# Gated linear attention: decay sums held in both signs, one VectorE operation per level for differences and one for factors, none on GpSimd

## The chip, the core and the metric

The kernel runs on one core of a Trainium2 chip. The metric is the device time of one execution in microseconds (us). TensorE (PE) multiplies matrices, VectorE (DVE), ScalarE (ACT) and GpSimd (POOL) work element by element on 128 partitions, and SyncE (SP) issues most of the DMAs. The engines run side by side, each through its own queue in order, and wait for each other by semaphores.

## The reference, cut to what matters

The network has several layers of 256 tokens by 1024 columns: gated linear attention, a convolutional FFN, sparse attention, a second FFN, a mixer and an expert layer. Only the first is touched. It computes, in float32:

```python
def gla_mixer(h, w_in, w_alpha_up, b_alpha, g_out, w_o):      # H=4 heads, DK=128, DV=256, chunks of C=64
    q, k, v, r, a_low = jnp.split(h @ w_in, splits, axis=-1)
    log_a = log_sigmoid(a_low @ w_alpha_up + b_alpha) / 16.0
    ...
    def step(state, inp):
        q_, k_, v_, g_ = inp                                   # q_ already times DK ** -0.5
        b = jnp.cumsum(g_, axis=2)
        o_inter = einsum('bhtk,bhkv->bhtv', q_ * exp(b), state)
        diff = b[:, :, :, None, :] - b[:, :, None, :, :]
        decay = where(causal, exp(minimum(diff, 0.0)), 0.0)
        att = einsum('bhtk,bhsk,bhtsk->bhts', q_, k_, decay)
        o_intra = einsum('bhts,bhsv->bhtv', att, v_)
        b_last = b[:, :, -1:, :]
        new_state = state * exp(b_last) + einsum('bhsk,bhsv->bhkv', k_ * exp(b_last - b), v_)
        return new_state, o_inter + o_intra
    ...
    o = o * rsqrt(mean(o * o) + EPS) * g_out
    return (o * silu(r)) @ w_o
```

So the attention weight of token t on an earlier token s is the sum over the 128 key channels of q[t] k[s] exp(b[t] - b[s]), where b is the running sum of the log decays.

## The kernel before, in words

All weights are streamed from memory in units of 128x1024 floats. Each unit is brought by one DMA into one of 4 buffers `raw`. ScalarE rounds it into `whi` (line 273), VectorE takes the rest `wlo = raw - whi` (line 274), and TensorE multiplies with three matmuls for each piece (lines 284 to 286). There are 5 buffers `whi` and 5 `wlo`. Whatever VectorE does besides stands in the same queue as these subtractions.

`gla` first multiplies the 8 units of `gla_a`, which give k and q, kept transposed in the tile `qk` (line 731, one head at a time: channels on the partitions, tokens along the row, first the four heads of k, then those of q). Then come the 12 units of `gla_b`, in groups of 4 with a PSUM bank for each half of the tokens: units 4 to 7 give the second half of v, 8 to 15 give r.

Between these units stands the attention, as steps of a background generator. The decay sums `b` come from `decays` (scans at line 714). The pairs of tokens are then split into levels, with blocks of m = 128, 64, 32, 16, 8, 4, 2 and 1 tokens: at level m a token s in the first block of a pair of blocks meets a token t in the second one, and the decay between them is the product of two factors taken against the last token r of the first block. For each level,

- `decay(m)` takes two VectorE differences of 128x512 elements: `r - b` on first blocks (line 725), `b - r` on second blocks (line 726); ScalarE then takes the exponential of the whole 128x1024 tile (line 727);
- two GpSimd multiplications of 128x512 put k on first blocks (line 791) and q on second blocks (line 792);
- `products(m)` multiplies first by second blocks on TensorE (line 767 for m = 128, 774 for m = 64, 782 below), and copies the result into the matrix `att`, by ScalarE for the first two levels and by VectorE's copy with a mask (line 783) for the others and for the diagonal (m = 0, which needs no decay).

The differences run 2 levels ahead of the factors, and the products follow 3 levels behind them. When all levels are in `att`, it is multiplied with v (lines 807 and 808). Line 741 multiplies silu(r) with a gain, on GpSimd too.

The code names engines and buffers. The order within an engine's queue, and the waits, come from a scheduler that goes by its own costs, so a change of an operation's shape or engine can move its neighbours. The places touched are line 681 (the tile `b`), lines 692 to 697 (views), 714, 719 to 727, 741, and 790 to 792.

Of the kernel before, what the change touches and what calls it, by code (L numbers as in the profile page):

```python
# [13 lines left out]
AF = mybir.ActivationFunctionType  # L14
ALU = mybir.AluOpType
# [5 lines left out]
T = 256  # L21
# [166 lines left out]
class Net:  # L188
# [479 lines left out]
    def gla(self):  # L668
        nc = self.nc
        with ExitStack() as es:  # L670
            sp = self.pool("gla", es)
# [4 lines left out]
            gg = self.t(sp, [128, D])  # L676
# [1 line left out]
            self.strict = False  # L678
            xh, xl = self.xh, self.xl
            qk = self.t(sp, [128, 2, 4, T])  # L680
            b = self.t(sp, [128, 4, T])
            aT = self.t(sp, [16, T])
            att = self.t(sp, [128, 8, 128])
            attx = self.t(sp, [128, 4, 128])
            ones = self.t(sp, [128, T])
# [3 lines left out]
            levels = (128, 64) + MASKED  # L689
            AHEAD, LAG = 2, 3  # L690
            E = {}
            bf = b.rearrange("p h t -> p (h t)")
            kf = qk[:, 0].rearrange("p h t -> p (h t)")
            qf = qk[:, 1].rearrange("p h t -> p (h t)")

            def view(a, m):
                return a.rearrange("p (n u m) -> p n u m", u=2, m=m)

            def decays():
                z = self.t(sp, [128, 4, T])  # L700
                mn = self.t(sp, [128, 4, T])
                for h2 in range(2):
                    pz = self.ps()
                    for j in range(2):
                        h = 2 * h2 + j
                        zs = pz[:, j * T:(j + 1) * T]
                        nc.tensor.matmul(zs, up[:, h * 128:(h + 1) * 128], aT, start=True, stop=True)
                        nc.scalar.activation(z[:, h], zs, AF.Abs, bias=ba[:, h:h + 1])
                        nc.vector.tensor_scalar(mn[:, h], zs, ba[:, h:h + 1], 0.0, op0=ALU.add, op1=ALU.min)
                nc.scalar.activation(z, z, AF.Exp, scale=-1.0)  # L710
                nc.scalar.activation(z, z, AF.Ln, bias=1.0)
                nc.vector.tensor_sub(z, mn, z)
                for h in range(4):
                    nc.vector.tensor_tensor_scan(b[:, h], ones, z[:, h], 0.0, op0=ALU.mult, op1=ALU.add)
                yield
                for m in levels[:AHEAD]:
                    decay(m)
                    yield

            def decay(m):  # L720
                n = 512 // m
                e = E[m] = self.t(sp, [128, 1024])
                ev, bv = view(e, m), view(bf, m)
                r = bv[:, :, 0, m - 1:m].to_broadcast([128, n, m])
                nc.vector.tensor_sub(ev[:, :, 0], r, bv[:, :, 0])  # L725
                nc.vector.tensor_sub(ev[:, :, 1], bv[:, :, 1], r)
                nc.scalar.activation(e, e, AF.Exp, scale=1.0 / 16.0)

            def evac_a(i, p):
# [2 lines left out]
            v = self.t(sp, [128, 2, D])  # L732
            rg = self.t(sp, [128, 2, D])

            def evac_b(g, ps):
                for t in range(2):
                    s = slice((g % 2) * 512, (g % 2) * 512 + 512)
                    to, fn = (v, AF.Copy) if g < 2 else (rg, AF.Silu)
                    nc.scalar.activation(to[:, t, s], ps[t], fn, scale=self.rs[:, t:t + 1])
                    if g == 2:  # L740
                        nc.gpsimd.tensor_mul(rg[:, t, s], rg[:, t, s], gg[:, s])
            evac_b(0, self.rest())
            p = self.ps()
            self.unit_n(self.A["gla_n"], 32, xh, xl, p[:, :T])
            self.tick()
            nc.vector.tensor_copy(aT, p[32:48, :T])
            nc.vector.tensor_add(aT, p[:16, :T], aT)
            nc.vector.tensor_mul(aT, aT, self.rw[:16])
            self.bg.append(decays())
            self.run(self.gemm_w(self.A["gla_a"], xh, xl, T, evac_a))  # L750
            self.close_right()
# [6 lines left out]
            def products(m):  # L758

                if m == 0:  # L760
                    kk, qq = qk[:, 0], qk[:, 1]
                else:
                    kk = qq = E[m].rearrange("p (h t) -> p h t", h=4)
                if m == 128:
                    p = self.ps()
                    for h in range(4):
                        nc.tensor.matmul(p[:, h * 128:(h + 1) * 128], kk[:, h, :128], kk[:, h, 128:], start=True, stop=True)
                    nc.scalar.activation(attx.rearrange("p h t -> p (h t)"), p, AF.Copy)
                elif m == 64:
                    p = self.ps()  # L770
                    for t in range(2):
                        for h in range(4):
                            i, s = t * 4 + h, t * 128
                            nc.tensor.matmul(p[:64, i * 64:(i + 1) * 64], kk[:, h, s:s + 64], kk[:, h, s + 64:s + 128], start=True, stop=True)
                    nc.scalar.activation(att[:64, :, 64:], p[:64].rearrange("p (i t) -> p i t", i=8), AF.Copy)
                else:
                    mask = self.cc(f"m{m}", "cg") if m else self.ident
                    for t in range(2):
                        p = self.ps()
                        for h in range(4):  # L780
                            s = slice(t * 128, t * 128 + 128)
                            nc.tensor.matmul(p[:, h * 128:(h + 1) * 128], kk[:, h, s], qq[:, h, s], start=True, stop=True)  # L782
                        nc.vector.copy_predicated(att[:, t * 4:t * 4 + 4], mask[:, None, :].bitcast(U32).to_broadcast([128, 4, 128]),  # L783
                                                  p.rearrange("p (h t) -> p h t", h=4))

            def attention():
                for i, m in enumerate(levels):
                    if i + AHEAD < len(levels):
                        decay(levels[i + AHEAD])
                    ev = view(E[m], m)  # L790
                    nc.gpsimd.tensor_mul(ev[:, :, 0], ev[:, :, 0], view(kf, m)[:, :, 0])
                    nc.gpsimd.tensor_mul(ev[:, :, 1], ev[:, :, 1], view(qf, m)[:, :, 1])
                    if i >= LAG:
                        products(levels[i - LAG])
                    yield
                for m in levels[len(levels) - LAG:] + (0,):
                    products(m)
                    yield
                po, r = {}, {}
                for t in range(2):  # L800
                    for h2 in range(2):
                        p = po[t, h2] = self.ps()
                        for j in range(2):
                            h = 2 * h2 + j
                            o = p[:, j * 256:(j + 1) * 256]
                            if t:
                                nc.tensor.matmul(o, attx[:, h], v[:, 0, h * 256:(h + 1) * 256], start=True, stop=False)
                            nc.tensor.matmul(o, att[:, t * 4 + h], v[:, t, h * 256:(h + 1) * 256], start=not t, stop=True)
                            sq = self.t(sp, [128, 256], tag="sq", bufs=2)
                            nc.scalar.activation(sq, o, AF.Square, accum_out=ss[:, t * 4 + h:t * 4 + h + 1])  # L810
                    r[t] = self.root(sp, ss[:, 4 * t:4 * t + 4], 4, 1.0 / 256)
                    yield

                def heads(t, hs, by):
                    for h in hs:
                        s = slice(h * 256, (h + 1) * 256)
                        nc.vector.scalar_tensor_tensor(on[:, t, s], po[t, h // 2][:, (h % 2) * 256:(h % 2 + 1) * 256], r[t][:, h:h + 1],
                                                       by[:, s], op0=ALU.mult, op1=ALU.mult)
                for t in range(2):
                    heads(t, (0, 1), rg[:, t])  # L820
                    self.turn_half(on[:, t, :512], oh, ol, 0, t * 128)
                    yield
                for t in range(2):
                    heads(t, (2, 3), gg)
                yield

            self.bg.append(attention())
            self.run(self.gemm_t(self.A["gla_b"][4:8], xh, xl, self.TT, lambda g, ps: evac_b(1, ps)), lambda: self.tick(2))
            self.run(self.gemm_t(self.A["gla_b"][8:], xh, xl, self.TT, lambda g, ps: evac_b(g + 2, ps)))
            self.drain()  # L830
            for t in range(2):
# [1058 lines left out]
```

## Time and profile before

| | |
|---|---|
| median of 3 runs | 1677.5 us (1676.87 to 1677.64) |
| the profiled execution, its own time | 1678.32 us |
| its span, first to last instruction | 1676.5 us |
| granted TensorE clock, mean of the span | 0.995 |
| TensorE busy | 1645.5 us (98%) |
| VectorE busy | 1271.6 us (76%) |
| ScalarE busy | 870.0 us (52%) |
| GpSimd busy | 99.3 us (6%) |

Start times in the views are counted from the start of the span. The busy time of one instruction includes some overlap with the next one on its engine: where several follow each other without a gap, the distance between their starts is what one of them costs the queue. In the views, unnamed tiles are all called `v`. "Releaser" is what ended an idle time.

### The profile page before, as it was taken

The page shows a single profiled execution, that of the slowest core. Times are in us where ns is not written, and L with a number is a line of the kernel's source. Part 1 is how long each engine was busy: PE and PEld are TensorE (multiplying, and loading weights), DVE is VectorE, ACT ScalarE, POOL GpSimd, SP SyncE. Part 2 cuts the span into 40 slices and gives each one's busy share as a digit, 9 for nine tenths or more (in the row PEclk, how much of TensorE's full clock was granted, in tenths as well). Part 3 has the DMA queues.
Part 4 walks back from the last instruction along what each step waited for, and adds up shares of the span by engine and source line. Part 5 has one row for each costly group of instructions (what it writes and reads, how often), then busy time and mean ns, then how long its engine had stood idle before and what let it go on. Part 6 is the DMA issues. An engine that isn't in the chain of part 4 may idle for free.

```text
span 1676.5 us, 28909 instructions
## 1 busy us (share of the span) xinstructions
PE 1645.5 (98%) x11363; PEld 1467.6 (88%) x11363; DVE 1271.6 (76%) x2168; ACT 870.0 (52%) x1379; POOL 99.3 (6%) x106
## 2 busy tenths in 40 slices
PE   9899999999999999999999999999999999999999
PEld 7688998898788998789779999999988998778887
DVE  6956987598857986599668889999955449985554
ACT  7445665456646665467455445433444444344443
POOL 0710000011101000210010000000000000000000
PEclk9899999999999999999999999999999999999999
DMA  7436656554215666554154555644555554465553
GB/s 244 136 110 215 186 183 186 162 183 153 73 47 179 196 186 188 162 168 151 63 178 162 189 181 171 192 159 155 175 186 188 185 186 134 136 208 189 189 189 112
DMA packets 76952, 278.16 MB, mean 166 GB/s; under 512 B 8688, under 2 KB 9072, under 8 KB 76688
## 3 DMA queue, kind: packets, MB, share of 16 engines
q1 hardware_dynamic: 74736, 269.39, 50.2%
q10 hardware_dynamic: 2080, 6.94, 1.2%
q8 instruction: 89, 1.46, 0.3%
q14 instruction: 47, 0.39, 0.1%
HBM read 275.24 MB, written 1.05 MB: 165 GB/s over the span
## 4 chain that ended last, share of the span: by engine, by line
PE 74%; issue 13%; DVE 10%; ACT 1%; POOL 1%; DMA 0%; SPq 0%; DVEq 0%; POOLq 0%; ACTq 0%
PE ps L286 22%; PE ps L284 22%; PE ps L285 22%; DVE wlo L274 3%; PE ps L935 2%; PE ps L1688 1%; PE ps L1014 1%; DVE H L1693 1%; DVE A L1674 1%; PE ps L1449 1%; DVE v L725 0%; PE ps L395 0%; DVE ru L952 0%; PE ps L292 0%; PE ps L782 0%
## 5 line engine op out<-in xcount | busy, mean ns | idle before, releaser
L274 DVE TENSOR_TENSOR wlo<-raw,whi 128x1024 fp32r<-128x1024 f32 (+1 forms) x504 | 622.9, 1243 | 224.3 <-ACT whi L273 223.4
L273 ACT ACTIVATE whi<-raw 128x1024 fp32r<-128x1024 f32 (+1 forms) x510 | 536.8, 1054 | 470.8 <-PE ps L285 269.3
L284 PE MATMUL ps<-xth,whi 128*128 128x256 f32 (+1 forms) x1960 | 553.5, 282 | 0.0
L286 PE MATMUL ps<-xth,wlo 128*128 128x256 f32 (+1 forms) x1960 | 552.3, 282 | 0.3 <-DVE wlo L274 0.3
L285 PE MATMUL ps<-xtl,whi 128*128 128x256 f32 (+1 forms) x1960 | 552.0, 282 | 0.0
L284 PEld LDWEIGHTS ps<-xth,whi 128*128 128x128 f32 x1960 | 370.9, 189 | 1.9 <-issue 1.5
L286 PEld LDWEIGHTS ps<-xth,wlo 128*128 128x128 f32 x1960 | 371.1, 189 | 0.5 <-DVE wlo L274 0.5
L285 PEld LDWEIGHTS ps<-xtl,whi 128*128 128x128 f32 x1960 | 369.0, 188 | 0.2
L285 PE MATMUL ps<-wlo,Wh 128*128 128x512 f32 x512 | 200.9, 397 | 0.7
L286 PE MATMUL ps<-whi,Wl 128*128 128x512 f32 x512 | 198.8, 395 | 0.0
L284 PE MATMUL ps<-whi,Wh 128*128 128x512 f32 x512 | 194.8, 396 | 0.0
L279 ACT ACTIVATE Wh<-H 128x256 fp32r<-128x256 f32 x128 | 53.1, 416 | 169.1 <-PE ps L285 167.5
L284 PE MATMUL ps<-whi,xth 128*128 128x512 f32 x288 | 119.0, 413 | 3.8 <-DVE v L783 3.8
L286 PE MATMUL ps<-whi,xtl 128*128 128x512 f32 x288 | 116.1, 405 | 1.8 <-DVE xtl L280 1.6
L285 PE MATMUL ps<-wlo,xth 128*128 128x512 f32 x288 | 115.7, 402 | 2.2 <-DVE wlo L274 2.1
L286 PEld LDWEIGHTS ps<-whi,Wl 128*128 128x128 f32 x512 | 96.2, 188 | 22.7
L284 PEld LDWEIGHTS ps<-whi,Wh 128*128 128x128 f32 x512 | 96.3, 188 | 22.5
L285 PEld LDWEIGHTS ps<-wlo,Wh 128*128 128x128 f32 x512 | 95.2, 188 | 22.1 <-DVE wlo L274 1.3
L280 DVE TENSOR_TENSOR Wl<-H,Wh 128x256 fp32r<-128x256 f32 x128 | 54.0, 423 | 56.7 <-ACT Wh L279 56.7
L286 PEld LDWEIGHTS ps<-whi,xtl 128*128 128x128 f32 x288 | 55.3, 192 | 16.1 <-DVE xtl L280 2.9
L284 PE MATMUL ps<-whi,v 128*128 128x512 f32 x176 | 69.3, 394 | 0.0
L284 PEld LDWEIGHTS ps<-whi,xth 128*128 128x128 f32 x288 | 55.4, 192 | 15.8 <-DVE v L783 4.0
(401 smaller groups left out, 2045.2 us busy)
## 6 DMA issues: line engine op xcount, KB each, us to landing
raw<-in_p_u SPq DMA_DIRECT2D x128, 512.0 KB, 3.7
raw<-in_p_v SPq DMA_DIRECT2D x128, 512.0 KB, 3.5
raw<-in_up SPq DMA_DIRECT2D x80, 512.0 KB, 3.7
raw<-in_dn SPq DMA_DIRECT2D x44, 512.0 KB, 3.6
raw<-in_m_t SPq DMA_DIRECT2D x20, 512.0 KB, 3.6
raw<-in_gla_b SPq DMA_DIRECT2D x16, 512.0 KB, 4.1
raw<-in_p_q SPq DMA_DIRECT2D x12, 512.0 KB, 4.8
raw<-in_m_w SPq DMA_DIRECT2D x9, 512.0 KB, 3.5
```

What stands on the lines that cost most here:

```text
L273: self.q(nc.scalar.activation(hi[:, c], raw[:, c], AF.Copy))
L274: self.q((eng or nc.vector).tensor_sub(lo[:, c], raw[:, c], hi[:, c].bitcast(F32)))
L279: self.q(self.nc.scalar.activation(hi, src, AF.Copy))
L280: self.q(self.nc.vector.tensor_sub(lo, src, hi.bitcast(F32)))
L284: nc.tensor.matmul(o, lh, rh, start=first, stop=False)
L285: nc.tensor.matmul(o, lh, rl, start=False, stop=False)
L286: nc.tensor.matmul(o, ll, rh, start=False, stop=last)
L935: mm = lambda o, l, rr, first=False, last=False: nc.tensor.matmul(o, l, rr, start=first, stop=last, skip_group_check=True)
L1014: nc.tensor.matmul(ph[:, :256], xx[i].rearrange("p (m s) -> p m s", s=8)[:, i:i + 128, jj % 8], w[v][:, j * 256:(j + 1) * 256], start=jj = ...
L1449: mm = lambda o, l, rr, first=False, last=False: nc.tensor.matmul(o, l, rr, start=first, stop=last, skip_group_check=True)
L1674: nc.vector.tensor_mul(two(a, nn), two(eq, nn), each(gTs[i], ts, nn))
L1688: nc.tensor.matmul(p[:, t * nn:(t + 1) * nn], B[:, 8 * h + t], Ap[i][:, 8 * h + t], start=i == 0, stop=i == 1)
```

## The change

The tile `b` becomes twice as large and holds the sums in both signs: the scans write the second half, and one ScalarE operation (line 725 of the changed kernel) writes the negated sums into the first half. A view `pairs` then walks, for every pair of blocks, over the first block in the first half of the tile and the second block in the second half: of `b` this is -b on first blocks and +b on second blocks, of `qk` it is k on first and q on second blocks. Its companion with `last=True` repeats the pair's reference token, -r and then +r. Subtracting the one from the other gives both differences of a level in one VectorE operation of 128x1024, and one VectorE multiplication of 128x1024 puts both factors on. The 8 tiles of the levels become 7 buffers in turn, so that the last level (m = 1) takes the buffer of the first one (m = 128). The multiplication of silu(r) with its gain goes to VectorE as well.

```diff
-            b = self.t(sp, [128, 4, T])
+            b = self.t(sp, [128, 2, 4, T])
...
-            def view(a, m):
-                return a.rearrange("p (n u m) -> p n u m", u=2, m=m)
+            def blocks(e, m):
+                return e.rearrange("p (n u m) -> p n u m", u=2, m=m)
+
+            def pairs(a, m, last=False):
+                n = 512 // m
+                f = a.rearrange("p w h t -> p w (h t)")
+                v = f.rearrange("p w (n u m) -> p n w u m", u=2, m=m)
+                if last:
+                    return v[:, :, :, 0, m - 1:m].to_broadcast([128, n, 2, m])
+                r = v[:, :, :, 0]
+                ap = [list(x) for x in r.ap]
+                ap[2][0] += m
+                return bass.AP(r.tensor, r.offset, ap)
...
                 for h in range(4):
-                    nc.vector.tensor_tensor_scan(b[:, h], ones, z[:, h], 0.0, op0=ALU.mult, op1=ALU.add)
+                    nc.vector.tensor_tensor_scan(b[:, 1, h], ones, z[:, h], 0.0, op0=ALU.mult, op1=ALU.add)
+                nc.scalar.activation(b[:, 0], b[:, 1], AF.Copy, scale=-1.0)
                 yield
...
             def decay(m):
-                n = 512 // m
-                e = E[m] = self.t(sp, [128, 1024])
-                ev, bv = view(e, m), view(bf, m)
-                r = bv[:, :, 0, m - 1:m].to_broadcast([128, n, m])
-                nc.vector.tensor_sub(ev[:, :, 0], r, bv[:, :, 0])
-                nc.vector.tensor_sub(ev[:, :, 1], bv[:, :, 1], r)
+                e = E[m] = self.t(sp, [128, 1024], tag="E", bufs=7)
+                nc.vector.tensor_sub(blocks(e, m), pairs(b, m), pairs(b, m, True))
                 nc.scalar.activation(e, e, AF.Exp, scale=1.0 / 16.0)
...
-                        nc.gpsimd.tensor_mul(rg[:, t, s], rg[:, t, s], gg[:, s])
+                        nc.vector.tensor_mul(rg[:, t, s], rg[:, t, s], gg[:, s])
...
-                    ev = view(E[m], m)
-                    nc.gpsimd.tensor_mul(ev[:, :, 0], ev[:, :, 0], view(kf, m)[:, :, 0])
-                    nc.gpsimd.tensor_mul(ev[:, :, 1], ev[:, :, 1], view(qf, m)[:, :, 1])
+                    nc.vector.tensor_mul(blocks(E[m], m), blocks(E[m], m), pairs(qk, m))
```

The queues of the changed kernel, as built, show what moved. First VectorE, from the subtraction of the second unit of v to that of the fourth. `v_255` is `b`, `v_254` is `qk`, `v_642`, `v_648`, `v_678` and `v_694` are the tiles of levels 8, 4, 2 and 1. Before:

```order
L274 TENSOR_TENSOR wlo_627<-raw_624,whi_626 128x1024
L725 TENSOR_TENSOR v_642<-v_255 128x64x8
L726 TENSOR_TENSOR v_642<-v_255 128x64x8
L731 SCALAR_TENSOR_TENSOR v_254<-ps_550,v_233 128x256
L725 TENSOR_TENSOR v_648<-v_255 128x128x4
L726 TENSOR_TENSOR v_648<-v_255 128x128x4
L274 TENSOR_TENSOR wlo_663<-raw_660,whi_662 128x1024
L725 TENSOR_TENSOR v_678<-v_255 128x256x2
L726 TENSOR_TENSOR v_678<-v_255 128x256x2
L725 TENSOR_TENSOR v_694<-v_255 128x512
L726 TENSOR_TENSOR v_694<-v_255 128x512
L274 TENSOR_TENSOR wlo_715<-raw_712,whi_714 128x1024
```

In the changed kernel the same stretch of VectorE's queue begins after the differences of levels 8 and 4. The `E` tiles are, in the order in which they are multiplied here, the levels 128, 64, 32, 16, 8 and 4; `E_669` and `E_683` are levels 2 and 1:

```order
L797 TENSOR_TENSOR E_382<-E_382,v_254 128x1024
L797 TENSOR_TENSOR E_417<-E_417,v_254 128x1024
L797 TENSOR_TENSOR E_611<-E_611,v_254 128x1024
L797 TENSOR_TENSOR E_615<-E_615,v_254 128x1024
L733 TENSOR_TENSOR E_669<-v_255 128x1024
L797 TENSOR_TENSOR E_637<-E_637,v_254 128x1024
L733 TENSOR_TENSOR E_683<-v_255 128x1024
L797 TENSOR_TENSOR E_641<-E_641,v_254 128x1024
L790 COPY_PREDICATED v_257<-v_250,ps_687 128x512
L790 COPY_PREDICATED v_257<-v_250,ps_693 128x512
L274 TENSOR_TENSOR wlo_702<-raw_699,whi_701 128x1024
```

Ahead of these rows stands the subtraction of the third unit (`wlo_654`). Where four small differences stood between the subtractions of the third and the fourth unit of v (`wlo_663` and `wlo_715` before, `wlo_654` and `wlo_702` now), there are now two differences, six multiplications and two masked copies. The masked copies of levels 16 and below, which stood behind five subtractions of weights before, now stand between them.

Second, TensorE, from the products of level 64 to the fourth unit of v. `ps_592` and `ps_593` are the two banks of v; `v_417` and `v_612` are levels 64 and 32. Before:

```order
L774 MATMUL ps_684<-v_417 64x64 x8
L782 MATMUL ps_700<-v_612 128x128 x4
L782 MATMUL ps_706<-v_612 128x128 x4
L284 MATMUL ps_592<-whi_714,xth_81 128x512
L285 MATMUL ps_592<-wlo_715,xth_81 128x512
L286 MATMUL ps_592<-whi_714,xtl_82 128x512
```

TensorE's queue at the same place of the changed kernel, where the banks of v are `ps_591` and `ps_592`:

```order
L781 MATMUL ps_673<-E_417 64x64 x8
L789 MATMUL ps_687<-E_611 128x128 x4
L789 MATMUL ps_693<-E_611 128x128 x4
L284 MATMUL ps_591<-whi_701,xth_81 128x512
L284 MATMUL ps_592<-whi_701,xth_81 128x512
L789 MATMUL ps_718<-E_615 128x128 x4
L789 MATMUL ps_724<-E_615 128x128 x4
L789 MATMUL ps_731<-E_637 128x128
L285 MATMUL ps_591<-wlo_702,xth_81 128x512
```

The products of level 16, and the first of level 8, have moved into the fourth unit, between its first two matmuls (which need only `whi`) and the first one that needs `wlo_702`. The rest of the queue holds the same matmuls, with the products of a level at most one unit away from where they stood.

## Rows read from the trace of the kernel before

**Rows 1.** The page's slices: busy tenths of two engines in 40 equal parts.
```profile
DVE  6956987598857986599668889999955449985554
POOL 0710000011101000210010000000000000000000
```

**Rows 2.** Busy time by stretch: stretch, length, each engine's busy (count), PEclk, DMA, GB/s.
```profile
40.00:80.00 40.00, 32.44 (x199) 27.58 (x198) 40.00 (x35) 18.05 (x20) 30.14 (x16) 0.91 0.39 123
48.60:101.45 52.85, 45.28 (x246) 37.64 (x245) 44.52 (x39) 20.92 (x23) 29.74 (x16) 0.90 0.41 129
...
60.00:64.00 4.00, 4.00 (x10) 3.15 (x10) 4.00 (x3) 1.01 (x2) 4.00 (x3) 0.50 0.46 133
```

**Rows 3.** Waits of TensorE, 30 to 120 us: in total, times, longest.
```profile
PE ps L284 <- DVE v L783: 3.8, 1, 3.8
PE ps L285 <- DVE wlo L274: 2.1, 2, 1.4
PE ps L767 <- POOL v L792: 1.5, 1, 1.5
```

**Rows 4.** Timeline of TensorE: start, us, engine, line, what, count, [idle before].
```profile
48.60 0.40 PE L284 MATMUL ps<-whi,xth 128*128 128x512 f32 x1
...
51.38 0.39 PE L284 MATMUL ps<-whi,xth 128*128 128x512 f32 x1
...
56.88 1.16 PE L767 MATMUL ps<-v 128*128 128x128 f32 x8 [1.51 <-POOL v L792]
57.79 0.47 PE L284 MATMUL ps<-whi,xth 128*128 128x512 f32 x1
...
64.64 1.61 PE L774 MATMUL ps<-v 128*64 128x64 f32 x16
66.18 2.05 PE L782 MATMUL ps<-v 128*128 128x128 f32 x16
...
96.90 1.95 PE L782 MATMUL ps<-v 128*128 128x128 f32 x16
101.45 1.02 PE L808 MATMUL ps<-v,v 128*128 128x256 f32 x4
```

**Rows 5.** Timeline of VectorE, 36 to 112 us.
```profile
39.99 0.40 DVE L731 SCALAR_TENSOR_TENSOR v<-ps,v 128x256 f32<-128x256 f32 x1
40.30 0.68 DVE L725 TENSOR_TENSOR v<-v 128x512 f32<-128x512 f32 x1
...
59.52 1.75 DVE L725 TENSOR_TENSOR v<-v 128x512 f32<-128x512 f32 x1
...
62.88 1.75 DVE L725 TENSOR_TENSOR v<-v 128x512 f32<-128x512 f32 x1
...
66.22 11.84 DVE L274 TENSOR_TENSOR wlo<-raw,whi 128x1024 fp32r<-128x1024 f32 x5
...
84.32 0.75 DVE L783 COPY_PREDICATED v<-v,ps 128x512 f32<-128x512 uint32 x1 [1.36 <-PE ps L782]
84.95 1.22 DVE L274 TENSOR_TENSOR wlo<-raw,whi 128x1024 fp32r<-128x1024 f32 x1
86.08 0.75 DVE L783 COPY_PREDICATED v<-v,ps 128x512 f32<-128x512 uint32 x1
```

**Rows 6.** Timeline of GpSimd, the same stretch.
```profile
55.18 7.23 POOL L792 TENSOR_TENSOR v<-v,v 128x512 f32<-128x512 f32 x4 [1.56 <-DVE v L731]
62.37 1.72 POOL L791 TENSOR_TENSOR v<-v,v 128x512 f32<-128x512 f32 x1
...
76.94 2.50 POOL L792 TENSOR_TENSOR v<-v,v 128x512 f32<-128x512 f32 x1
```

**Rows 7.** Timeline of ScalarE.
```profile
31.75 1.06 ACT L710 ACTIVATE v<-v 128x1024 f32<-128x1024 f32 x1
32.72 1.05 ACT L273 ACTIVATE whi<-raw 128x1024 fp32r<-128x1024 f32 x1
...
72.19 1.06 ACT L273 ACTIVATE whi<-raw 128x1024 fp32r<-128x1024 f32 x1 [3.37 <-DMA raw<-in_gla_b]
```

More of the change, by code (lines that the diff above doesn't have):

```diff
@@ L691, in gla @@
             E = {}
-            bf = b.rearrange("p h t -> p (h t)")
-            kf = qk[:, 0].rearrange("p h t -> p (h t)")
-            qf = qk[:, 1].rearrange("p h t -> p (h t)")
-            def view(a, m):
-                return a.rearrange("p (n u m) -> p n u m", u=2, m=m)
+            def blocks(e, m):
[10 more added lines that the diff above has]
+                return bass.AP(r.tensor, r.offset, ap)
             def decays():
```

## The prediction

> **What bounds the kernel now.** I read the slices first, because the average (VectorE busy 76%) says nothing about one stage. GpSimd is busy almost only in slices 2 and 3, and there VectorE stands at 9 [rows 1]. From 40 to 80 us VectorE is busy for all 40.00 us and GpSimd for 30.14; TensorE, which bounds the rest of the kernel, has only 32.44, at a granted clock of 0.91 [rows 2]. So in this stage VectorE is the limit, and TensorE waits: 7.4 us in four waits for VectorE's subtractions, VectorE's masked copies and GpSimd's factors [rows 3]. Behind such waits the clock fell as well: from 60 to 64 us it was 0.50, the lower of its two levels (1.2 GHz), so the ten matmuls there took twice their time [rows 2].
>
> TensorE's own timeline [rows 4] says what the stage would need without this. The units of v begin at 48.60 and the first product with v (line 808) at 101.45: 52.85 us. Between them stand 9 units of 12 matmuls, 2.78 each (48.60 to 51.38); the products of level 128, 0.91 (56.88 to 57.79); of level 64, 1.54 (64.64 to 66.18); and 7 pairs of products for the masked levels and the diagonal, 1.77 each (96.90 to 101.45 is a pair and a unit, 4.55). That is 25.0 + 0.9 + 1.5 + 12.4 = 39.9. So 13.0 of the 52.85 us are waits and low clock, and what VectorE can return is at most that.
>
> **Why VectorE is slow there.** A difference of 128x512 costs the queue 0.60 alone (0.68 busy at 40.30), but four of them from 59.52 to 66.22 took 1.68 each. Subtractions of 128x1024 cost 1.13 alone (84.95 to 86.08), and five from 66.22 took 11.84, 2.37 each [rows 5]. The additions, 1.08 and 1.24, are about the length of one GpSimd multiplication, and GpSimd's own rhythm in these stretches is the same: 7.23 for four, 1.72, later 2.50 [rows 6]. The two engines take turns: each VectorE operation with two inputs pays for a GpSimd operation. Behind the last GpSimd multiplication (76.94 plus 2.50) VectorE is back at 1.13.
>
> **The change part by part.** Removed: 16 differences of 128x512 and 16 GpSimd multiplications, with them the taking of turns. Added on VectorE: 8 differences and 8 multiplications of 128x1024. The trace has no such two-row walk. Its nearest row is the subtraction of 128x1024 with two inputs, 1.13 alone; the highest row of that shape is 2.37. Lower than 1.13 I do not go, as 512 elements cost 0.60 and 1024 cost 1.13, about 1 ns for an element whatever the operation. I take 1.13 and keep 2.37 as the other end.
>
> Walk down VectorE's new queue with these prices. The scans and a scaling of q end at 40.30 (0.31 for a scaling, 39.99 to 40.30 [rows 5]). A subtraction of weights follows until 41.43. Beside it ScalarE writes the negated sums: 128x1024, 0.97 from start to start (31.75 to 32.72 [rows 7]), from about 40.0 to 41.0. So this added operation and its wait cost nothing; without that cover they would cost 1.0. From 41.43 to the end of the subtraction for the fifth unit of TensorE's stretch (`wlo_750`) stand 16 new operations at X each, 5 subtractions at 1.13, 4 scalings at 0.31 and 6 masked copies at 0.63 (84.32 to 84.95 [rows 5]). The end is 41.43 + 5.65 + 1.24 + 3.78 + 16 X = 52.1 + 16 X, 70.2 for X = 1.13. From there TensorE has the rest of that unit (2.32), four more units and three pairs to line 808: 2.32 + 11.12 + 5.31 = 18.75. So by VectorE line 808 comes at 70.85 + 16 X, which is 88.9.
>
> By TensorE it comes at 48.60 + 39.9 = 88.5 plus what it must still wait. In order: the first two units to 54.16; level 128 needs its factors, the first multiplication in VectorE's queue. Before it stand six differences (6.78), three subtractions (3.39) and four scalings (1.24); with its own 1.13 it is done at 41.43 + 12.54 = 53.97, in time. The next unit and level 64 run to 59.4; their factors are done by 55.1. Level 32 needs 56.2, level 16 needs 57.4, level 8 needs 59.7: all ahead of TensorE. The fourth unit needs its subtraction (`wlo_702`) at 63.5, and VectorE has it at 64.3, behind six multiplications and two masked copies: 0.8 late. For the fifth unit TensorE asks at 70.7, VectorE has it at 70.2. From there VectorE has a subtraction and two copies, 2.4, for each unit and pair of TensorE's, 4.55, and waits itself. So line 808 comes at 88.5 + 0.8 and 0.1 for handing over, 89.4 instead of 101.45: 12.0 us earlier.
>
> What else could be late? The 7 buffers make the last difference (level 1) wait for the products of level 128; these end at 55.1, and the difference comes at 59.7. The exponentials cost ScalarE 0.97 each; it is busy for 18.05 of 40 us [rows 2], and stands idle between them. A transfer may start when the subtraction four units earlier is done. One made ScalarE wait for 3.37 at 72.19 [rows 7]; now `wlo_702` frees its buffer at 64.3 for a unit that TensorE asks for behind 82. The multiplication of silu(r), two times 0.60 on VectorE, stands between the last copies, where VectorE idles for TensorE (1.36 at 84.32 [rows 5]): nothing. Behind line 808 the queues hold the same work in the same order, and TensorE is at its limit, so the 12.0 us stay. From the profiled execution's 1678.32 that gives 1666.3; the median of the runs was 0.8 less, so 1665.5.
>
> **The rivals.** *The walk costs more at small blocks.* At m = 1 the new operations read single words, alternately from two rows 4096 bytes apart. In its favour: VectorE's slack is only 0.5 us, so each addition counts in full. Against it: the old differences of level 1 also step over every second word, and at 62.88 took 1.75, no longer than level 2's at 59.52 with 1.75 [rows 5]; but these steps stay within a row. By the highest row the two operations of level 1 add 2 times 1.24: line 808 at 91.4, 1667.5. If level 2 pays too, 93.9 and 1670.0. The Trainium skill speaks for this rival: "Vector Engine (DVE) Microarchitecture Reference", section "Measured stream behaviour on trn2 (trn3 not measured)", has full rate only for runs of two adjacent words or more, and 1.76 ns instead of 1.05 for an element when both sources hop by 4 KiB at every element. By that figure, an estimate, level 1 adds 2 times 0.7, and the time would be 1666.4. No run here shows it yet.
>
> *Another wait takes the place.* Subtractions now end in bursts, so transfers start in bursts, and two units may come as late as the one at 72.19. Two waits of 3.37 in full make 1672.2. Against it: the DMA share of the stretch is 0.39 [rows 2].
>
> *Slower than before.* The turns are not what makes VectorE slow from 52 to 78, but the traffic of the stage itself; then operations of 128x1024 keep 2.37 there. With X = 2.37 line 808 comes at 70.85 + 37.9 = 108.8, 7.3 later than before: 1684.8. It decides from X = 1.91 on, where 70.85 + 16 X passes 101.45. For it speaks only that 9 us of multiplications are put on the engine that is already full. Against it: 1.13 at once behind GpSimd's last operation, with TensorE, ScalarE and DMA going on. The Trainium skill has a rule on this side, "Perfetto Trace Analysis", section "Optimizing Scalar/DVE Operations": with VectorE saturated, offloading to ScalarE or even GpSimd may make sense, which is what the change takes back. The same section warns that the two share a port, so that moving work between them might not help; rows 5 and 6 agree with the warning.
>
> **How the numbers follow.** The forecast, 1665.5, has 0.62. The costlier walk has 0.22 (1666.4 to 1670.0), the late transfers 0.06, slower 0.06; 0.04 remain for a smaller change that none of these names. Downwards there is little: without the 0.8 wait, and with level 64 at full clock, 1664. The range is 1664 to 1670.5. About 0.2% (3.4 us) is what a measurement can tell from no change: faster 0.90, same 0.04, slower 0.06.
>
> **What would show it.** In the changed profile VectorE's operations of 128x1024 start 1.13 apart from 45 to 64 us; TensorE's waits for VectorE and GpSimd there shrink from 7.4 to about 1; the clock shows no 0.50; line 808 starts near 89.4, and everything behind it is shifted by the same amount. The forecast is wrong if the new operations cost over 1.2 on average, or if line 808 comes early and the gain is lost behind it.

## The result, and the profile after

| | before | changed |
|---|---|---|
| median (lowest to highest, runs) | 1677.18 us (1676.85 to 1677.64, 4) | 1666.78 us (1665.43 to 1667.22, 4) |
| ratio, 95% interval | | 0.9936 (0.9925 to 0.9948) |
| profiled execution, its span, mean clock | 1678.32, 1676.5, 0.995 | 1665.43, 1663.7, 0.999 |

The change saves 10.4 us, 0.6%. Five more runs of it on another chip gave 1665.51 (1664.94 to 1666.59) against 1677.12 there. The forecast was 1665.5, in a range of 1664 to 1670.5.

TensorE's timeline of the changed kernel answers to [rows 4]; the columns are the same. The first row is the first unit of v, the last one the first product with v.

```profile
47.24 0.40 PE L284 MATMUL ps<-whi,xth 128*128 128x512 f32 x1
...
56.81 1.15 PE L781 MATMUL ps<-E 128*64 128x64 f32 x16
57.88 2.05 PE L789 MATMUL ps<-E 128*128 128x128 f32 x16
...
63.50 0.50 PE L285 MATMUL ps<-wlo,xth 128*128 128x512 f32 x1 [1.09 <-DVE wlo L274]
...
88.54 1.02 PE L813 MATMUL ps<-v,v 128*128 128x256 f32 x4
```

The stage takes 88.54 - 47.24 = 41.30 us instead of 52.85: 11.55 saved. From line 808 to the end of the span it was 1676.5 - 101.45 = 1575.05 before; now it is 1663.7 - 88.54 = 1575.16. So nothing is gained or given back behind the stage. What is left of the difference between the two profiles, 1.36, lies ahead of it (48.60 against 47.24) and is no part of the gain: ScalarE's operation of line 710 starts at 31.75 before [rows 7] and 1.36 earlier, at 30.39, in the changed kernel, where nothing that was changed has run yet.

Busy time by stretch, with the columns of [rows 2]: 40 to 80, the whole stage, and the four microseconds in which the clock was 0.50 before.

```profile
40.00:80.00 40.00, 38.89 (x257) 34.39 (x256) 38.72 (x42) 21.62 (x23) 0.00 (x0) 1.00 0.46 145
47.24:88.54 41.30, 40.19 (x247) 34.65 (x246) 38.11 (x41) 19.44 (x22) 0.00 (x0) 1.00 0.47 153
60.00:64.00 4.00, 2.91 (x22) 2.63 (x21) 4.00 (x5) 1.06 (x1) 0.00 (x0) 1.00 0.00 0
```

TensorE is busy for 38.89 of 40 us instead of 32.44, at full clock throughout (2.4 GHz), even in the stretch that holds its one wait. The waits of TensorE between 30 and 120 us, which answer to [rows 3], are two; below them stands the row of the kernel before that answers to the second:

```profile
PE ps L285 <- DVE wlo L274: 1.1, 1, 1.1
PE ps L395 <- DVE v L837: 0.7, 1, 0.7
```
```profile
PE ps L395 <- DVE v L832: 0.7, 1, 0.7
```

The first is the one that the walk foresaw; the second lies behind the stage and was there before. VectorE's timeline, for [rows 5]:

```profile
50.48 1.22 DVE L274 TENSOR_TENSOR wlo<-raw,whi 128x1024 fp32r<-128x1024 f32 x1
51.62 4.62 DVE L797 TENSOR_TENSOR E<-E,v 128x1024 f32<-128x1024 f32 x4
56.16 1.22 DVE L733 TENSOR_TENSOR E<-v 128x1024 f32<-128x1024 f32 x1
57.29 1.22 DVE L797 TENSOR_TENSOR E<-E,v 128x1024 f32<-128x1024 f32 x1
58.43 1.51 DVE L733 TENSOR_TENSOR E<-v 128x1024 f32<-128x1024 f32 x1
59.87 1.21 DVE L797 TENSOR_TENSOR E<-E,v 128x1024 f32<-128x1024 f32 x1
...
65.75 1.50 DVE L797 TENSOR_TENSOR E<-E,v 128x1024 f32<-128x1024 f32 x1
67.17 1.34 DVE L790 COPY_PREDICATED v<-v,ps 128x512 f32<-128x512 uint32 x2
```

From start to start the subtraction costs 1.14, four multiplications 4.54, the difference of level 2 (56.16) 1.13. Only level 1 is dearer: its difference 1.44 (58.43 to 59.87), its factors 1.42 (65.75 to 67.17).

### The profile page after: what moved, and what is told of

It is laid out like the page before. It is cut to its first block, busy times and chain, and to the rows that moved or that the text cites. A ratio compares the mean times of both kernels' runs of the same rounds, so it can differ in the third digit from the quotient of the medians.

```text
span 1663.7 us, 28890 instructions
## 1 busy us (share of the span) xinstructions
PE 1639.3 (99%) x11363; PEld 1463.7 (88%) x11363; DVE 1265.4 (76%) x2170; ACT 871.6 (52%) x1380; POOL 66.5 (4%) x88
## 4 chain that ended last, share of the span: by engine, by line
PE 64%; issue 24%; DVE 9%; ACT 1%; POOL 1%; DVEq 0%; POOLq 0%; ACTq 0%
PE ps L286 18%; PE ps L285 18%; PE ps L284 18%; DVE wlo L274 3%; PE ps L940 2%; PE ps L1693 1%; PE ps L1019 1%; DVE H L1698 1%; DVE A L1679 1%; PE ps L1454 1%; PE ps L789 1%; DVE ru L957 0%; POOL nv L424 0%; ACT whi L273 0%; PE ps L1725 0%
## 5 line engine op out<-in xcount | busy, mean ns | idle before, releaser
L274 DVE TENSOR_TENSOR wlo<-raw,whi 128x1024 fp32r<-128x1024 f32 (+1 forms) x504 | 613.1, 1223 | 223.8 <-ACT whi L273 222.6
L284 PE MATMUL ps<-whi,v 128*128 128x512 f32 x176 | 69.3, 394 | 0.0
L285 PE MATMUL ps<-wlo,v 128*128 128x512 f32 x176 | 69.0, 392 | 0.0
L286 PE MATMUL ps<-whi,v 128*128 128x512 f32 x176 | 69.0, 392 | 0.0
```

The lines of the kernel that those rows point to most:

```text
L274: self.q((eng or nc.vector).tensor_sub(lo[:, c], raw[:, c], hi[:, c].bitcast(F32)))
L284: nc.tensor.matmul(o, lh, rh, start=first, stop=False)
L285: nc.tensor.matmul(o, lh, rl, start=False, stop=False)
L286: nc.tensor.matmul(o, ll, rh, start=False, stop=last)
```

## The experiments

**The factors on VectorE, nothing merged.** The kernel before with one edit:

```diff
-                    nc.gpsimd.tensor_mul(ev[:, :, 0], ev[:, :, 0], view(kf, m)[:, :, 0])
-                    nc.gpsimd.tensor_mul(ev[:, :, 1], ev[:, :, 1], view(qf, m)[:, :, 1])
+                    nc.vector.tensor_mul(ev[:, :, 0], ev[:, :, 0], view(kf, m)[:, :, 0])
+                    nc.vector.tensor_mul(ev[:, :, 1], ev[:, :, 1], view(qf, m)[:, :, 1])
```

> The kernel before with one edit: the 16 factor multiplications of 128x512 go from GpSimd to VectorE. No negated sums, no merged walks. Theory (the taking of turns with GpSimd is what VectorE pays): two differences and two multiplications of 128x512 cost 4 x 0.60 = 2.40 us per level against 2 x 1.13 = 2.26 merged, so nearly all of the gain is there. The queue as built has the third subtraction of v late (58.1 against 55.3 asked for by TensorE) and the fourth by 1.1, so the first product with v comes near 92.4 us on the clock of the profile before: 1668 to 1671 us, 128x512 operations 0.60 apart. Rival (the merging of two operations into one walk is what pays): 1674 us or more.

Measured: 1665.78 us (1665.37 to 1666.57, 5 runs), against 1677.23 for the kernel before on that chip, ratio 0.9932 (0.9918 to 0.9945). So the change of engine alone gives all that the whole change gives. My number was too high by 2 us or more, because I had kept TensorE's order of the changed kernel. TensorE's timeline of this run shows the order that the scheduler chose here:

```profile
47.39 0.40 PE L284 MATMUL ps<-whi,xth 128*128 128x512 f32 x1
...
53.75 0.71 PE L284 MATMUL ps<-whi,xth 128*128 128x512 f32 x2
54.39 1.15 PE L774 MATMUL ps<-v 128*64 128x64 f32 x16
55.46 0.49 PE L782 MATMUL ps<-v 128*128 128x128 f32 x2
57.14 0.50 PE L285 MATMUL ps<-wlo,xth 128*128 128x512 f32 x1 [1.18 <-DVE wlo L274]
...
88.49 1.02 PE L808 MATMUL ps<-v,v 128*128 128x256 f32 x4
```

The third subtraction of v is late as foreseen. But the products of level 64 and the first of level 32 now stand ahead of the matmul that needs it, and fill most of the delay; 1.18 is left. For the fourth, which I had 1.1 late, TensorE did not wait at all. The stage took 88.49 - 47.39 = 41.10 us.

**The merged factors on GpSimd.** The changed kernel with one edit:

```diff
-                    nc.vector.tensor_mul(blocks(E[m], m), blocks(E[m], m), pairs(qk, m))
+                    nc.gpsimd.tensor_mul(blocks(E[m], m), blocks(E[m], m), pairs(qk, m))
```

> The changed kernel with one edit: the merged factor multiplication of 128x1024 goes back to GpSimd. Differences stay merged on VectorE. Theory: GpSimd holds VectorE up again, 8 operations of about 2.4 us, and the factors are ready only near 79 us: most of the gain is lost, 1673 us or more, VectorE's subtractions of 128x1024 there 2.3 us or more apart. Rival (merging pays): 1669 us or less.

Measured: 1673.05 us (1671.64 to 1674.2, 10 runs), ratio 0.9974 (0.9964 to 0.9983) to before. Some 7 us of the gain are lost by the change of engine, as the theory has it. Its second half, how they are lost, was wrong in part. GpSimd's timeline (the rows overlap, as each gives a group of operations from its first one on), VectorE's, and TensorE's wait:

```profile
51.13 14.87 POOL L797 TENSOR_TENSOR E<-E,v 128x1024 f32<-128x1024 f32 x3 [29.23 <-DVE v L738]
58.83 21.20 POOL L797 TENSOR_TENSOR E<-E,v 128x1024 f32<-128x1024 f32 x7
65.96 14.07 POOL L797 TENSOR_TENSOR E<-E,v 128x1024 f32<-128x1024 f32 x5
```
```profile
50.90 1.22 DVE L274 TENSOR_TENSOR wlo<-raw,whi 128x1024 fp32r<-128x1024 f32 x1
52.03 1.22 DVE L733 TENSOR_TENSOR E<-v 128x1024 f32<-128x1024 f32 x1
53.17 3.49 DVE L274 TENSOR_TENSOR wlo<-raw,whi 128x1024 fp32r<-128x1024 f32 x3
61.09 1.52 DVE L733 TENSOR_TENSOR E<-v 128x1024 f32<-128x1024 f32 x1 [4.44 <-PE ps L774]
...
66.09 3.30 DVE L274 TENSOR_TENSOR wlo<-raw,whi 128x1024 fp32r<-128x1024 f32 x1 [2.33 <-ACT whi L273]
```
```profile
PE ps L774 <- POOL E L797: 5.5, 1, 5.5
```

Three subtractions follow each other at 1.13 beside a GpSimd instruction that has begun. That first one lasts until 58.83, 7.7 us, and the shortest of the eight takes 2.34: here it was GpSimd that was held up, until VectorE had nothing ready. TensorE then waits 5.5 for the factors of level 128, about what that instruction lost (7.7 less 2.34). Behind the wait the granted clock was 0.50 from 57 to 60 us, and the stage took 95.33 - 47.66 = 47.67 us, 6.4 more than in the changed kernel. Later subtractions take 3.30 and 2.45, so VectorE waits there too. (The difference of level 1 at 61.09 waited for the buffer of level 128, whose products were late; in the changed kernel it did not wait.)

**Idle GpSimd work, reading or only writing.** The changed kernel with operations that nobody needs, started by the negated sums. The order of the other engines is that of the changed kernel, row by row. First with two inputs:

```diff
                 nc.scalar.activation(b[:, 0], b[:, 1], AF.Copy, scale=-1.0)
+                nc.gpsimd.tensor_copy(rg[:, 1, :1], b[:, 0, 0, :1])
+                for _ in range(16):
+                    nc.gpsimd.tensor_mul(rg[:, 1, :512], gg[:, :512], gg[:, 512:])
```

> The changed kernel with 16 added GpSimd multiplications of 128x512, two inputs from on-chip memory, into a part of a tile that nobody needs yet; they start when the negated sums are there, near 41 us, and nobody waits for them. The order of all other engines is unchanged. Theory: each takes its turn with a two-input VectorE operation, 1.08 us, so VectorE loses up to 17 us in a stage where it has 0.5 us to spare: 1677 to 1684 us, operations of 128x1024 about 2.3 apart while GpSimd is busy. Rival (the traffic of the stage made VectorE slow): 1667 us, 1.13 apart.

Measured: 1684.2 us (1682.94 to 1685.08, 4 runs), slower than before (ratio 1.004, 1.0025 to 1.0055), just above the upper end (1684) of what the theory said. GpSimd, VectorE, and the waits of TensorE:

```profile
42.18 35.70 POOL L728 TENSOR_TENSOR v<-v 128x512 f32<-128x512 f32 x16
```
```profile
60.95 8.93 DVE L800 TENSOR_TENSOR E<-E,v 128x1024 f32<-128x1024 f32 x4
69.80 2.29 DVE L736 TENSOR_TENSOR E<-v 128x1024 f32<-128x1024 f32 x1
72.01 2.30 DVE L800 TENSOR_TENSOR E<-E,v 128x1024 f32<-128x1024 f32 x1
```
```profile
PE ps L285 <- DVE wlo L274: 8.1, 2, 6.0
PE ps L777 <- DVE E L800: 4.6, 1, 4.6
```

A multiplication on VectorE costs 2.21 instead of 1.13 while GpSimd is busy, and a GpSimd one 35.70 / 16 = 2.23: they go in step. The addition, 1.08, is what I had read from the rows of before. Then the same with fills, which write but read nothing:

```diff
+                nc.gpsimd.tensor_copy(rg[:, 1, :1], b[:, 0, 0, :1])
+                for _ in range(32):
+                    nc.gpsimd.memset(rg[:, 1], 0.0)
```

> The changed kernel with 32 added GpSimd fills of 128x1024 (written, nothing read) in the place of the multiplications of the run before, from about 41 us on. If any GpSimd operation takes a turn with VectorE: 1677 us or more. If only one that reads on-chip memory does: 1667 us, VectorE's operations 1.13 apart beside a busy GpSimd. I hold the second for likelier (0.7), as the Trainium skill has it (SBUF — State Buffer, section Who interferes with whom).

Measured: 1665.91 us (1664.58 to 1667.29, 4 runs), the same as the changed kernel (1666.78 and 1665.51).

```profile
42.00 32.32 POOL L728 MEMSET v<- 128x1024 f32 x32
```
```profile
53.35 4.62 DVE L800 TENSOR_TENSOR E<-E,v 128x1024 f32<-128x1024 f32 x4
57.90 1.22 DVE L736 TENSOR_TENSOR E<-v 128x1024 f32<-128x1024 f32 x1
```

GpSimd is busy for 32 us on end, and VectorE's operations keep 4.55 for four. So neither the stage's traffic nor a GpSimd that is merely busy slows VectorE, but GpSimd operations that read; ones with a single input were not tried. This is a rule of the Trainium skill's "SBUF — State Buffer", section "Who interferes with whom": an instruction of VectorE with two on-chip inputs contends with a GpSimd one that reads, not with one that only writes.

**Level 1 without the change of rows.** One profiled run of the changed kernel, level 1 alone in the old form:

```diff
-                nc.vector.tensor_sub(blocks(e, m), pairs(b, m), pairs(b, m, True))
+                if m == 1:
+                    ev, bv = blocks(e, m), blocks(b[:, 1].rearrange("p h t -> p (h t)"), m)
+                    nc.vector.tensor_sub(ev[:, :, 0], bv[:, :, 0], bv[:, :, 0])
+                    nc.vector.tensor_sub(ev[:, :, 1], bv[:, :, 1], bv[:, :, 0])
+                else:
+                    nc.vector.tensor_sub(blocks(e, m), pairs(b, m), pairs(b, m, True))
...
-                    nc.vector.tensor_mul(blocks(E[m], m), blocks(E[m], m), pairs(qk, m))
+                    if m == 1:
+                        for w in range(2):
+                            ev, s = blocks(E[m], m)[:, :, w], blocks(qk[:, w].rearrange("p h t -> p (h t)"), m)[:, :, w]
+                            nc.vector.tensor_mul(ev, ev, s)
+                    else:
+                        nc.vector.tensor_mul(blocks(E[m], m), blocks(E[m], m), pairs(qk, m))
```

> The changed kernel with level 1 alone in the old form: two differences and two factors of 128x512 that step over every second word of one row each, instead of one walk that changes between two rows at every word (that walk took 1.44 and 1.42 from start to start, the other levels 1.13). If changing rows at every word is what costs the 0.3 us, the four operations take 0.60 each, 2.40 together. If any access to single words costs it, 0.75 each, 3.0 together.

```profile
58.51 0.70 DVE L735 TENSOR_TENSOR E<-v 128x512 f32<-128x512 f32 x1
59.12 0.70 DVE L736 TENSOR_TENSOR E<-v 128x512 f32<-128x512 f32 x1
59.72 1.23 DVE L807 TENSOR_TENSOR E<-E,v 128x1024 f32<-128x1024 f32 x1
...
65.59 1.29 DVE L805 TENSOR_TENSOR E<-E,v 128x512 f32<-128x512 f32 x2
66.80 1.37 DVE L795 COPY_PREDICATED v<-v,ps 128x512 f32<-128x512 uint32 x2
```

The differences cost 0.61 and 0.60, the two factors 1.21: 2.42 together instead of 2.86. Steps of two words within a row cost nothing more; it is the change of rows at every word that costs 0.3 us per operation. TensorE's wait in the stage is 0.64 there instead of 1.09. The run took 1665.13 us, which one run can't set apart from 1665.51.

**A better version: the residual's subtraction.** The changed profile still shows GpSimd and VectorE against each other in the residuals of the three mixers. GpSimd's row and VectorE's at the first of them, and TensorE's wait:

```profile
124.45 2.38 POOL L274 TENSOR_TENSOR wlo<-raw,whi 128x1024 fp32r<-128x1024 f32 x1
```
```profile
124.51 3.53 DVE L431 SCALAR_TENSOR_TENSOR xn<-v,nr,v 128x512 f32<-128x512 f32 x2 [1.91 <-POOL nr L419]
```
```profile
PE ps L395 <- DVE xn L431: 1.5, 1, 1.5
```

Two scalings that take 1.42 where GpSimd is idle (at 133.42 in the same run) take 3.53, and TensorE waits 1.48 for the first. The changed kernel, with that subtraction on VectorE:

```diff
-                    lu.append(n.unit(lead[0][len(lu)], n.nc.gpsimd if c == "v" else None))
+                    lu.append(n.unit(lead[0][len(lu)]))
```

> The changed kernel with one more GpSimd operation class taken away: in the residual of the three mixers one weight subtraction of 128x1024 (2.38 us on GpSimd) starts just ahead of the scaling of the normed rows and holds its first operation, which should take 0.65, for 2.8; TensorE then waits 1.48 us, at three places. Here VectorE does that subtraction behind the scalings. Theory (turns): each wait of 1.48 goes, a part comes back because one more subtraction of 1.13 stands before the splits: 1 to 1.5 us per place, 1662.4 to 1664 us. Rival (these waits are set by something else, the root before them): no change, 1666.8.

Measured: 1663.01 us (1662.98 to 1664.16, 5 runs), 2.5 less than the changed kernel on the same chip (1665.51). VectorE, then TensorE's waits from 118 to 140 us:

```profile
126.25 1.41 DVE L431 SCALAR_TENSOR_TENSOR xn<-v,nr,v 128x512 f32<-128x512 f32 x2 [1.92 <-POOL nr L419]
127.58 3.48 DVE L274 TENSOR_TENSOR wlo<-raw,whi 128x1024 fp32r<-128x1024 f32 x3
130.99 0.68 DVE L280 TENSOR_TENSOR xtl<-ps,xth 128x512 fp32r<-128x512 f32 x1
```
```profile
PE ps L286 <- DVE xtl L280: 1.3, 1, 1.3
```

The wait of 1.48 is gone, and 0.7 of it comes back, so a mixer gives 0.8 where I had expected 1 to 1.5: three subtractions now stand in a row before the split of the next rows (line 280), for which TensorE waited 0.6 before and 1.3 now. The same edit in the kernel of the first experiment, with nothing merged:

> The kernel of the first experiment (before, with the factors as halves on VectorE, nothing merged) with the residual's subtraction on VectorE as well. If merging is worth nothing on its own, the same as the run before it, 1662 to 1664 us; if merging is worth its 0.14 us per level and the two operations of level 1 cost nothing extra, 1 us or more behind it.

Measured: 1662.31 us (1661.45 to 1662.59, 4 runs), ratio 0.9907 (0.9892 to 0.9923) to before on that chip. It is the fastest of all, ahead of the merged version by 0.7 us in runs that do not overlap, and it has neither negated sums nor merged walks. In the two profiles 0.2 of that lies in the stage (89.02 - 47.93 = 41.09 against 90.29 - 48.97 = 41.32). It can't be told from these runs whether level 1 or the order of the queues makes the 0.7.

## Why the prediction was right

- *VectorE is the bound of this stage, and GpSimd makes it so.* Shown: 16 idle multiplications on GpSimd take back more than the whole gain; 32 fills take back nothing. That VectorE's operation always pays for GpSimd's was too simple: in the second experiment GpSimd paid first. One reading of the rows was wrong without touching the sums: VectorE stands at 9 in slice 2 alone, slice 3 shows 5, and of GpSimd's 99.3 us only 30.14 lie between 40 and 80 us.
- *New operations at 1.13.* Right for levels 128 to 2. Level 1's took 1.44 and 1.42, so the term of 16 times 1.13 was 0.6 too small. The rival of the costlier walk had its mechanism right, and its price, 1.24 per operation by the highest row, was four times too high. The estimate from the Trainium skill's figure, 0.7, was more than twice too high: the measurement decides.
- *The negated sums cost nothing.* Right: the first differences follow at 40.07 on the subtraction that began at 38.94, without idle time.
- *TensorE waits once, for the fourth subtraction, 0.8.* It waited there and nowhere else in the stage, so no late transfer took its place. The wait was 1.09, where the walk had 0.8 and 0.1 for handing over; level 1's difference, 0.3 dearer, stands before that subtraction.
- *12.0 us earlier.* It was 11.55 (41.30 for 52.85 of stage), and it stayed to the end. Of the 0.5 that is missing, 0.2 is the longer wait; the rest is TensorE's own time, 41.30 - 1.09 = 40.2 where the walk had 39.9. The forecast of 1665.5 lies 1.3 below the first median, 1666.78, and on the second, 1665.51. The mechanism is not luck, but a hit closer than about 1 us is: the two medians are of the same kernel, and between profiles of it the entry into the stage moves by more than was mis-sized: in the repeat of the changed kernel the first unit of v begins at 49.33 instead of 47.24, and the stage takes 41.33:

```profile
49.33 0.40 PE L284 MATMUL ps<-whi,xth 128*128 128x512 f32 x1
...
90.66 1.02 PE L813 MATMUL ps<-v,v 128*128 128x256 f32 x4
```

- *The clock.* The 0.50 of 60 to 64 us is gone, though TensorE has 2.91 of 4 us there. The prediction put its fall down to the waits, 7.4 in all before; the one wait of 1.09 did not lower it.
- *What was not said.* The prediction gave the gain to the parts of the change together. The first experiment shows that the merging, with its second copy of the sums and its ScalarE operation, has no share in it that these runs can tell: 1665.78 without, 1665.51 with.

## What to carry to other kernels

Before work is moved to GpSimd to spare VectorE, look at what each operation reads: where both take two inputs from on-chip memory, as here, GpSimd's operation costs VectorE (or the other way round) about its own length, and moving it back was free or better in both places tried here. In a timeline the sign is that operations of one shape cost one engine's price plus the other's, in step, only while both are busy. And where a queue is full, ask which waits the scheduler's new order fills before a late operation is charged: the first experiment was mis-sized by just that.

## What the runs showed of the hardware that was not expected

- Who waits for whom is not fixed. In the kernel before and under idle reads, the two engines went in step (1.68, 2.37 and 2.23 per pair); in the second experiment VectorE ran five operations at its own price while one GpSimd instruction stood for 7.7 us. In three places what began first went first: VectorE at 50.90 ahead of GpSimd at 51.13, GpSimd at 65.96 ahead of VectorE at 66.09, and in the mixer GpSimd at 124.45 ahead of VectorE at 124.51. That does not tell why VectorE's next four operations also went ahead of the first of these, where under the idle reads the two alternated. What decides it was not tried.
- On VectorE a float32 operand that steps over every second word of a row costs no more than a contiguous one (0.60 for 512 elements, as line 748's multiplication from 85.70 to 86.30); one that changes between two rows at every word costs 0.3 us more for 1024 elements, whether both inputs do so (1.44) or one (1.42).
